# Experts of a two-block model on one core: where the row weights are copied, which buffers the block outputs use, and when the last norm's rows are loaded

## The chip, the cores and the metric

The kernel runs on one core of one Trainium2 chip, in one launch. The core has a matrix engine (TensorE; PE in the profile, PEld for its weight loads), VectorE (DVE), ScalarE (ACT), GpSimd (POOL), and SyncE (SP), which here only issues DMAs. Each engine takes its own instructions strictly in the order in which they stand in its queue; engines and DMAs wait for each other through semaphores. The metric is device time in microseconds, less is better. The kernel before took 4433.74 us (median of 3 runs, 4425.26 to 4436.02).

## The reference, cut to what matters

The model is an attention block of two layers, then a block with a token mixer, two layer norms and a mixture of experts over 1024 tokens of 1024 features. The change is in the experts and in the last norm:

```python
def _moe_ffn(h, router_w, router_b, w1, w3, w2, sw1, sw3, sw2):
    scores = jax.nn.sigmoid((h @ router_w).astype(f32))
    ...                                     # 64 experts, 8 chosen for each token
    wts = wts / jnp.sum(wts, -1, keepdims=True) * ROUTED_SCALE
    ...                                     # tokens sorted by expert, blocks of rows
    def body(acc, blk):
        tok, wt, e = blk
        xb = h[tok]                                            # gather rows
        hid = jax.nn.silu(xb @ w1[e]) * (xb @ w3[e])
        return acc.at[tok].add(wt[:, None] * (hid @ w2[e])), None   # scatter, weighted
    shared = (jax.nn.silu(h @ sw1) * (h @ sw3)) @ sw2
    return routed.astype(h.dtype) + shared

x = _layernorm(DN_ALPHA * x + g2 * f, ln2_w[l], ln2_b[l])      # the last norm
```

All tensors are float32. A product is done as three products of rounded parts (high times high, low times high, high times low), so each operand is first split in two on ACT and DVE.

## The kernel before, in words

The experts' part starts near 3176 us of the profiled span and ends it. Its work is a list of 105 blocks of up to 128 rows: 8 blocks of the shared expert, then 97 blocks of the 64 routed experts, whose capacities by falling count are fixed (`CAPS`); a loop at the end would do what exceeds them. For each routed block the kernel does these steps:

- `gather` (L2558 on): a one-hot comparison on DVE and eight small matmuls give the rows' token numbers `ix`; an indirect DMA, issued by POOL (L2575), brings the rows with their 64 weights by expert from `h_d` into `xg`.
- behind it, in `come` (L2697, L2698): POOL copies the weights' column out of `xg` into `wc`.
- `turn` (L2578): eight transposes on PE, and the split of the rows into `xh` and `xl`.
- `first` (L2595): the product with w1 and w3, silu, product `hid`. A block of at most 64 rows packs both parts of its rows into one product, and its two halves are added by way of a buffer `both` (L2605 to L2607) with the tag `ye`.
- `middle` (L2613): transposes `hid` and splits it.
- `second` (L2623): the product with w2; ACT writes it, times `wc`, into `y`, also of tag `ye` (L2631); POOL issues an indirect DMA that adds the rows to `acc_d` (L2635).

The tag `ye` has two buffers for both uses, `ix` has six, `xg` three. A tile that is allocated anew waits until everything that uses its buffer is done; for `ye` and `ix` that is the landing of the scatter that reads them. Two scatters in a row touch the same tensor `acc_d`, so each one also waits for the landing of the one before.

The steps of different blocks are interleaved by the loop at L2715: in turn i come the rows of block i + 3, `first` of block i, `turn` of block i + 1, seven splits of the next experts' weights, `second` of block i - 1 and `middle` of block i. This is the order of the program; the order in an engine's queue is set by a scheduler, which puts instructions where it reckons that they can run. Only SP keeps the program's order in this part (L2681). SP loads the experts' weights (three loads of 1 MB an expert) into four buffers `w_raw`.

The last norm needs the modulation's last part `g2` as a row on all partitions (eight transposes and two copies, `mod_row`), and the two vectors `ln2_w` and `ln2_b`. They are made in turn 3 of the loop, in buffers of the pool `rp`, which holds the first norm's rows till then. That pool stays open to the end.

Of the kernel before, what the change touches and what calls it, by code (L numbers as in the profile page):

```python
# [39 lines left out]
class K:  # L40
    """Engines, pools and constants that all phases share."""
# [23 lines left out]
    def psum(self, **bufs):  # L65
        """Banks by what they are for."""
        if self._ps:
            self._ps.close()
        self._ps = ExitStack()
        self.bufs = bufs or dict(mm=5, tr=2, po=1)  # L70
        self.ps = self._ps.enter_context(self.tc.tile_pool(name="ps", bufs=1, space=PSUM, reuse_waits="tile"))
# [7 lines left out]
    def rsqrt(self, out, in_, scale, eps):  # L79
        """out = (in_ * scale + eps) ** -0.5"""  # L80
# [8 lines left out]
    def split(self, hi, lo, src, scale=None, eng=None):  # L89
        """hi + lo = src (* scale, one number per partition), hi rounded as the tensor engine does."""  # L90
# [9 lines left out]
    def mm3(self, out, a, b, start, stop):  # L100
        """out += a^T b with both operands in two parts."""
# [6 lines left out]
    def mm_packed(self, both, top, a2, ah, bh, bl, start, stop):  # L108
        """both += a2^T bh and top += ah^T bl; a2 has the two parts of a side by side, top is both's first half,
        and the sum of both's halves is a^T b."""  # L110
# [8 lines left out]
    def vectors(self, pool, name, rows):  # L119
        """Vectors from DRAM (each a multiple of P long) as columns [P, n]: {key: column range}."""  # L120
# [16 lines left out]
    def bcast_row(self, out, col):  # L137
        """out[:, j] = col[j] for every partition: a column of P numbers as a row on all partitions."""
# [5 lines left out]
def vec(ap):  # L144
    """A DRAM vector (n * P,) as rows [n, P]."""
    return ap.rearrange("(n p) -> n p", p=P)


def gemv(k, pool, out, cs, w, b, ncols, chunk=128, group=4, tag="mm", ttag="tr", bufs=4):
    """out[:, j, :] = w[:, j * P:(j + 1) * P]^T cs + b[:, j], cs [P, KD, 2]; in steps."""  # L150
# [22 lines left out]
def run(gen, n=None):  # L173
    """The next n steps of a generator, or all that are left."""
    while n is None or n > 0:
        if next(gen, run) is run:
            return
        n = n and n - 1
# [42 lines left out]
def beside(main, side, n):  # L221
    """Steps of main, with n of side after every one."""
# [16 lines left out]
def put_h(k, wp, xn, tok, hh, hl, g, sh, onv=2):  # L239
    """(xn * g + sh) for a token tile, transposed and in two parts; onv of four features' tiles on the vector  # L240
    engine."""
# [20 lines left out]
def load_w(k, pool, w, c0, n, kt=KD, scale=None, tag="w", wmax=P, ktmax=KD, bufs=2, rbufs=2, rpool=None):  # L262
    """Columns c0..c0+n of w [kt * P, :] in two parts, [P, kt, n]."""
# [12 lines left out]
def head_weights(k, pool, I, l, pr, v, own=None):  # L276
    """Weights of a pair of heads' queries, and of its keys and values, in two parts, scaled by the norms'; in the
    places of the input product's weights, the parts in the pool own if there is one."""
# [15 lines left out]
class Columns:  # L294
    """Weights' tiles of P columns one after another, in turns in two pools; the first may be loaded ahead."""
# [12 lines left out]
def product(k, w, h, t0, n):  # L308
    """A bank with w^T h over n tokens from t0 on."""
# [7 lines left out]
def silu_out(k, sg, ps, dst):  # L317
    """silu(ps) into DRAM by way of sg."""
# [16 lines left out]
def block1(k, I, x_open, x_out, ahead, fill):  # L335
    """The first block: both layers; x_open(pool), then x_out(pool, t, tile) for the x token tiles, and
    what x_open returns, each of which returns what is to be done later; ahead: the next
    block's first weights, then a product with them; fill(pool): steps to be done beside the second layer's attention."""
    nc, tc = k.nc, k.tc
    A = nc.vector  # L340
    with ExitStack() as es:
# [16 lines left out]
        def early(pool=None):  # L358
            """The second layer's first weights, then a product with them."""
# [7 lines left out]
        def vectors(l):  # L367
            """The layer's vectors and tables."""
# [21 lines left out]
        def modulation(l, gp, **kw):  # L390
            """Shift and scale, then the gate."""
# [11 lines left out]
        def second(gp, **kw):  # L403
            """What the second layer needs."""
# [13 lines left out]
        def begin(wp):  # L418
            """The first layer's input."""
# [25 lines left out]
        for l in range(2):  # L445
# [26 lines left out]
            def weights():  # L472
                """In the place of what only the preparations need: the output's weights."""
# [15 lines left out]
def in_proj(k, I, l, last, h, vecs, keep, wp, ydram, sga_d, begin):  # L489
    """The layer's input product and its two convolution branches; begin(pool) makes the input."""  # L490
# [5 lines left out]
    with ExitStack() as es:  # L496
# [6 lines left out]
        def each(c0, n, cks, fn):  # L503
            """fn(feature tile, chunk of tokens, PSUM) over columns c0..c0+n of the input's product."""
# [6 lines left out]
        # queries' and keys' low-rank inputs in two parts, and the sums of their squares per token  # L511
# [16 lines left out]
        def to_tokens(sm, n):  # L528
            """Numbers per token in both rows of sm, on the tokens' partitions [P, n / P]; sm is used again."""
# [16 lines left out]
        # both segments with room for the taps that reach over their ends  # L546
# [9 lines left out]
        # conformer branch's input  # L556
# [12 lines left out]
        # the second layer's first ones have begun in the first layer  # L569
# [15 lines left out]
        def conformer():  # L585
            """Long convolution, layer norm over the features, pointwise product."""
# [23 lines left out]
        def pointwise(s):  # L610
            # mean and variance on all partitions
# [46 lines left out]
        # k_rope: both parts of the weights side by side, summed by tokens  # L658
# [28 lines left out]
        # gates of the attention's output  # L687
# [5 lines left out]
        # short convolution branch: gates, then the input  # L693
# [35 lines left out]
        def short():  # L729
            """The last product, and the convolution one chunk behind."""  # L730
# [11 lines left out]
def attention(k, I, l, last, v, hw, tabs, keep, fp, kp, ydram, sga_d, side, after):  # L742
    """All heads; side's steps beside the first one's preparation, after's beside the last two heads, when keep and
    the pools fp and kp aren't needed any more."""
    nc, tc = k.nc, k.tc
    lo_t = CT if last else 0
    with ExitStack() as es:
# [10 lines left out]
        # keys' shared part: norm weight, rotation, squares  # L758
# [7 lines left out]
        def rotate(eng, o, x, tb, tmp):  # L766
            """o = rotation of the pairs (x[j], x[16 + j]), o may be x; tb has the tables, tmp two buffers."""
# [2142 lines left out]
```

## Time and profile before

| what | value |
|---|---|
| median of 3 runs | 4433.74 us |
| span of the profiled execution | 4414.7 us |
| what lies around the span, against the median | 19.0 us |
| PE, DVE, ACT, POOL busy, of the span | 92%, 65%, 45%, 28% |
| stage of the routed blocks that is read below | 3300 to 4325 us |

The span runs from the first to the last instruction of the program; the page gives no other time for the profiled execution, so that the launch around it is taken as the difference to the median. A busy share says how long an engine had an instruction in work. POOL's 28% holds neither the time in which it waits for a DMA that it has issued nor the time for which those behind it in its queue are held up by that.

### The profile page before, as it was taken

What the parts mean: (1) busy time and instruction counts of PE and PEld (TensorE: products, weight loads), DVE (VectorE), ACT (ScalarE), POOL (GpSimd) and SP (SyncE); (2) the same over time, 40 slices, a digit from 0 to 9 for tenths busy, and PEclk for the clock granted to TensorE, in tenths of its full rate; (3) what the DMA queues carried; (4) which work ended last, traced back from release to release, by engine and by line L of the source; (5) the groups of instructions that cost most, each with busy time, mean ns of one, the idle gap of its engine ahead of it and who ended that gap; (6) DMA issues with size and microseconds to landing.
All of it is one profiled execution on the core that took longest, in us unless ns stands there. A gap on an engine that the chain in (4) does not pass through costs nothing. (4 is left out here: it accounts for less than half of the span.)

```text
span 4414.7 us, 61941 instructions
## 1 busy us (share of the span) xinstructions
PE 4045.3 (92%) x22375; PEld 3077.3 (70%) x22376; DVE 2878.1 (65%) x5659; ACT 1983.2 (45%) x4292; POOL 1231.9 (28%) x1211
## 2 busy tenths in 40 slices
PE   7999899999998999999997999999898898899993
PEld 5787666667776666788785788777776566666672
DVE  4684577764745778646764555667776676776775
ACT  4122366653112766423443133433256566666664
POOL 1201133332101333321334331122313333343233
PEclk9999999999999999999997999899999999999996
DMA  6121400123123001334434411215368888888885
GB/s 187 34 64 43 123 13 13 33 83 107 41 61 102 11 10 36 121 117 129 126 118 136 122 34 33 74 44 189 110 228 264 242 265 247 256 276 264 269 274 165
DMA packets 371316, 558.81 MB, mean 127 GB/s; under 512 B 52126, under 2 KB 285056, under 8 KB 346048
## 3 DMA queue, kind: packets, MB, share of 16 engines
q1 hardware_dynamic: 335728, 432.81, 30.5%
q0 software_dynamic: 35280, 122.02, 10.7%
q8 instruction: 177, 2.90, 0.3%
q14 instruction: 131, 1.07, 0.1%
HBM read 438.42 MB, written 116.33 MB: 126 GB/s over the span
## 5 line engine op out<-in xcount | busy, mean ns | idle before, releaser
L95 DVE TENSOR_TENSOR wa_lo<-w_raw,wa_hi 128x512 fp32r<-128x512 f32 x520 | 338.1, 685 | 18.6 <-ACT wa_hi L94 17.8
L94 ACT ACTIVATE wa_hi<-w_raw 128x512 fp32r<-128x512 f32 x520 | 299.7, 626 | 59.9 <-PE mm L106 24.9
L104 PE MATMUL mm<-hh,w_hi 128*128 128x512 f32 (+1 forms) x848 | 320.0, 377 | 4.7 <-ACT h L256 4.7
L105 PE MATMUL mm<-hl,w_hi 128*128 128x512 f32 (+1 forms) x848 | 318.7, 376 | 0.0
L106 PE MATMUL mm<-hh,w_lo 128*128 128x512 f32 (+1 forms) x848 | 317.1, 374 | 0.0
L104 PE MATMUL mm<-wa_hi,xh 128*128 128x512 f32 (+3 forms) x632 | 268.0, 424 | 2.8 <-ACT xh L94 2.7
L106 PE MATMUL mm<-wa_hi,xl 128*128 128x512 f32 (+3 forms) x632 | 259.4, 410 | 3.6 <-DVE xl L95 3.6
L105 PE MATMUL mm<-wa_lo,xh 128*128 128x512 f32 (+3 forms) x632 | 261.3, 414 | 1.2 <-DVE wa_lo L95 1.2
L892 DVE TENSOR_REDUCE mx<-mm 128x1 f32<-128x512 f32 (+1 forms) x400 | 225.1, 587 | 53.2 <-PE mm L891 50.7
L926 ACT ACTIVATE pe<-mm 128x512 f32<-128x512 f32 (+1 forms) x336 | 193.2, 588 | 144.3 <-PE mm L106 115.5
L931 POOL TENSOR_TENSOR pl<-pe,ph 128x512 fp32r<-128x512 f32 x96 | 142.0, 1482 | 335.4 <-ACT ph L930 326.5
L931 DVE TENSOR_TENSOR pl<-pe,ph 128x512 fp32r<-128x512 f32 (+1 forms) x240 | 204.6, 864 | 38.1 <-ACT ph L930 36.8
L2698 POOL COPY wc<-xg 128x1 f32<-128x1 f32 (+5 forms) x97 | 79.6, 820 | 508.4 <-DMA xg<-h_d,ix 502.3
L2635 POOL DMA_INDIRECT acc_d<-ye,ix x97 | 168.7, 1740 | 182.5 <-ACT hidh L94 73.4
L159 PE MATMUL mm<-gemv_w,b_c_cs 128*2 128x128 f32 x1536 | 199.0, 286 | 10.2 <-DMA gemv_w<-in_w_mod_dram 7.1
L2631 ACT ACTIVATE ye<-mm,wc 128x512 f32<-128x512 f32 (+5 forms) x194 | 127.6, 680 | 176.7 <-DMA acc_d<-ye,ix 125.1
L595 DVE SCALAR_TENSOR_TENSOR acc<-zc,b_v,acc 128x512 f32<-128x512 f32 (+1 forms) x300 | 199.3, 713 | 1.5
L104 PEld LDWEIGHTS mm<-hh,w_hi 128*128 128x128 f32 x848 | 161.3, 190 | 40.1 <-issue 7.6
L105 PEld LDWEIGHTS mm<-hl,w_hi 128*128 128x128 f32 x848 | 161.4, 190 | 33.8 <-issue 7.0
L94 ACT ACTIVATE w_hi<-w_raw 128x1024 fp32r<-128x1024 f32 x61 | 64.6, 1059 | 262.5 <-PE mm L105 227.2
L106 PEld LDWEIGHTS mm<-hh,w_lo 128*128 128x128 f32 x848 | 161.2, 190 | 28.1 <-issue 0.4
L930 ACT ACTIVATE ph<-pe 128x512 fp32r<-128x512 f32 (+1 forms) x296 | 178.0, 625 | 4.1
(779 smaller groups left out, 11572.8 us busy)
## 6 DMA issues: line engine op xcount, KB each, us to landing
w_raw<-in_exp_w_dram SPq DMA_DIRECT2D x192, 1024.0 KB
w_raw<-in_w_in_dram SPq DMA_DIRECT2D x69, 512.0 KB
gemv_w<-in_w_mod_dram SPq DMA_DIRECT2D x48, 512.0 KB
gemv_w<-in_ada_w_dram SPq DMA_DIRECT2D x48, 512.0 KB
rec<-rec SPq DMA_DIRECT2D x64, 256.0 KB
wo_raw<-in_w_out_dram SPq DMA_DIRECT2D x20, 512.0 KB
y<-ydram SPq DMA_DIRECT2D x36, 256.0 KB
xt<-in_x_dram SPq DMA_DIRECT2D x16, 512.0 KB
```

Of the source, the lines that this page charges most:

```text
L94: nc.scalar.activation(hi, src, AF.Copy)
L95: eng.tensor_tensor(lo, src, f32(hi), op=OP.subtract)
L104: mm(out, ah, bh, start=start, stop=False)
L105: mm(out, ah, bl, start=False, stop=False)
L106: mm(out, al, bh, start=False, stop=stop)
L159: nc.tensor.matmul(ps[:2, c0:c0 + chunk], cs[:, kk], wt[:, kk], start=kk == 0, stop=kk == KD - 1)
L595: nc.vector.scalar_tensor_tensor(o, zc[:, ft, p0 + j:p0 + j + c[1]], v["cfw"][:, 2 * j + ft:2 * j + ft + 1], o, op0=OP.mult, op1=OP.add)
L892: nc.vector.tensor_reduce(mx[:, t, c:c + 1], ps[:, :n], axis=AX.X, op=OP.max)
L926: nc.scalar.activation(pe, ps, AF.Exp)
L930: nc.scalar.activation(ph, pe, AF.Copy)
L931: (nc.gpsimd if j % PLP == PLP - 1 else nc.vector).tensor_tensor(pl, pe, f32(ph), op=OP.subtract)
L2635: nc.gpsimd.indirect_dma_start(out=self.acc_d, out_offset=bass.IndirectOffsetOnAxis(ap=st.ix[:n, 0:1], axis=0), in_=y[:n], in_offset=None, ...
```

## The change

The copy of the row weights `wc` moves in the program from `come`, behind the gather, to `turn`, two loop turns later. The block outputs `y` get a pool of their own with four buffers, at the place of the pool `rp`, which is closed as soon as the late steps of the output product are done; `ye` keeps its two buffers for `both` alone. `ix` gets eight buffers. `g2` and the last norm's two vectors are made behind the loop, in buffers of the second product's weights. The rest of the diff drops comments and docstrings.

```diff
     def experts(self, x1, out):
-            g2 = rp.tile([P, D], F32, name="g2", tag="sc2")
-            last = []
-            def beside_shared():
-                run(self.mod_row(g2, 5, "tr"))
-                last.extend((self.row(rp, "ln1w", I["ln2_w_2"][0]), self.row(rp, "ln1b", I["ln2_b_2"][0])))
...
-                st.ix = xp.tile([P, 1], I32, name="ix", bufs=6)
+                st.ix = xp.tile([P, 1], I32, name="ix", bufs=8)
...
             def turn(st):
                 n = st.n
+                if st.r is not None:
+                    st.wc = xp.tile([P, 1], F32, name="wc", bufs=6)
+                    nc.gpsimd.tensor_copy(st.wc[:n], st.x[:n, D + st.r:D + st.r + 1])
...
             def second(st):
-                y = xp.tile([P, D], F32, name="ye")
+                y = yp.tile([P, D], F32, name="y")
...
                     gather(b, self.routes[3][:, :, b.r:b.r + 1], b.base)
-                    b.wc = xp.tile([P, 1], F32, name="wc", bufs=6)
-                    nc.gpsimd.tensor_copy(b.wc[:b.n], b.x[:b.n, D + b.r:D + b.r + 1])
...
             next(late)
+            self.row_s.close()
+            yp = pool("y", 4, side="right")
             come(blocks[2])
...
                 run(route, 2)
-                if i == 3:
-                    beside_shared()
             ms.close()
             x = [wp.tile([P, D], F32, name="x", tag=("wa_hi", "wa_lo")[t % 2], bufs=8) for t in range(8)]
             for t in range(8):
                 k.load(x[t], self.x2_d[t * P:t * P + P])
+            g2, lw, lb = (wp.tile([P, D], F32, name=n, tag=g, bufs=4)
+                          for n, g in (("g2", "wb_hi"), ("lw", "wb_lo"), ("lb", "wb_lo")))
+            for a, n in ((lw, "ln2_w_2"), (lb, "ln2_b_2")):
+                k.load(a, I[n][0].unsqueeze(0).to_broadcast([P, D]))
+            run(self.mod_row(g2, 5, "tr"))
```

POOL's queue in the middle of the routed blocks, before (DMA xg is a gather, DMA acc_d a scatter, in brackets the semaphores that are waited for; DMASW ones are those of POOL's own DMAs):

```order
L2635 DMA acc_d<-ye,ix 1152x1024 [waits DMASW1_49,Activation_49]
L2575 DMA xg<-h_d,ix 32x1088 [waits DVE_49,PE_49,Pool_49]
L2635 DMA acc_d<-ye,ix 1152x1024 [waits DMASW3_49,Activation_49]
L2698 COPY wc<-xg 32x1 [waits DMASW4_49]
L2575 DMA xg<-h_d,ix 112x1088 [waits DVE_49,PE_49,Pool_49]
L2698 COPY wc<-xg 112x1 [waits DMASW6_49]
L2635 DMA acc_d<-ye,ix 1152x1024 [waits DMASW5_49,Activation_49]
L2575 DMA xg<-h_d,ix 128x1088 [waits DVE_49,PE_49,Pool_49]
L2698 COPY wc<-xg 128x1 [waits DMASW0_49]
```

And the same piece of POOL's queue now:

```order
L2629 DMA acc_d<-y,ix 1152x1024 [waits DMASW1_49,Activation_49]
L2566 DMA xg<-h_d,ix 32x1088 [waits DVE_49,PE_49,Pool_49]
L2629 DMA acc_d<-y,ix 1152x1024 [waits DMASW3_49,Activation_49]
L2574 COPY wc<-xg 32x1 [waits DMASW4_49]
L2566 DMA xg<-h_d,ix 112x1088 [waits DVE_49,PE_49,Pool_49]
L2574 COPY wc<-xg 112x1 [waits DMASW6_49]
L2629 DMA acc_d<-y,ix 1152x1024 [waits DMASW5_49,Activation_49]
L2566 DMA xg<-h_d,ix 128x1088 [waits DVE_49,PE_49,Pool_49]
L2574 COPY wc<-xg 128x1 [waits DMASW0_49]
```

Nothing has moved: the copy stands at the same place behind its own gather, and each scatter still waits for the landing of the one before. Over the whole part POOL's queue has the same order of gathers, copies and scatters as before.

ACT's queue at a packed block of 32 rows, before (ye<-mm at L2606 is `both`, ye<-mm,wc the block's output):

```order
L94 ACTIVATE wa_hi<-w_raw 128x512
L2606 ACTIVATE ye<-mm 32x512 [waits DMASW7_49,PE_49,Activation_49]
L94 ACTIVATE xh<-mm 128x4x112 [waits PE_49] x2
L94 ACTIVATE wa_hi<-w_raw 128x512 x2
L2610 ACTIVATE hid<-ye 32x256 [waits DVE_49]
L94 ACTIVATE wa_hi<-w_raw 128x512 x2
L2631 ACTIVATE ye<-mm,wc 128x512 [waits PE_49,DMASW1_49,Activation_49,Pool_49]
```

And the same now:

```order
L94 ACTIVATE wa_hi<-w_raw 128x512
L2600 ACTIVATE ye<-mm 32x512 [waits PE_49]
L94 ACTIVATE xh<-mm 128x4x112 [waits DVE_49,PE_49]
L94 ACTIVATE xh<-mm 128x4x112 [waits PE_49]
L94 ACTIVATE wa_hi<-w_raw 128x512 x2
L2604 ACTIVATE hid<-ye 32x256 [waits DVE_49]
L94 ACTIVATE wa_hi<-w_raw 128x512 x2
L2625 ACTIVATE y<-mm,wc 128x512 [waits DMASW3_49,PE_49,Pool_49]
```

The copy into `both` no longer waits for a scatter; the output waits for the scatter of four blocks before, where it was one or two blocks.

DVE's queue ahead of the first gather, before (posr are the positions from the router, g a row of the modulation, oh the one-hot rows of the first gathers):

```order
L2515 COPY posr<-mm 128x64 x8
L2389 COPY g_28053<-mm 128x512 x2
L2563 TENSOR_TENSOR oh<-c_iota,posr 128x1024 x2
L2809 TENSOR_TENSOR w_raw<-es,w_raw 128x64
L2812 SCALAR_TENSOR_TENSOR w_raw<-w_raw 128x64 x2
```

And now:

```order
L2506 COPY posr<-mm 128x64 x8
L2554 TENSOR_TENSOR oh<-c_iota,posr 128x1024 x2
L2806 TENSOR_TENSOR w_raw<-es,w_raw 128x64
L2809 SCALAR_TENSOR_TENSOR w_raw<-w_raw 128x64 x2
L2814 TENSOR_SCALAR w_raw<-w_raw 128x1
```

The two copies of `g2` are gone from there; they, the eight transposes, and on SP the two loads of the last norm's vectors stand at the end now, the loads behind those of `x`.

## Rows read from the trace of the kernel before

**Rows 1.** Stage 3300 to 4325: busy us of PE, PEld, DVE, ACT, POOL; clock, DMA share, GB/s.
```profile
3300.00:4325.00 1025.00, 914.46 (x4722) 681.99 (x4722) 717.88 (x1446) 641.92 (x1181) 362.30 (x274) 0.94 0.84 260
```

**Rows 2.** Waits of all engines, 3300 to 4325: us in total, times, longest.
```profile
POOL wc L2698 <- DMA xg<-h_d,ix: 455.3, 75, 10.5
ACT ye L2631 <- DMA acc_d<-ye,ix: 114.9, 31, 13.8
DVE ix L2573 <- DMA acc_d<-ye,ix: 97.8, 22, 8.2
...
PE mm L2620 <- DVE hid L2611: 56.2, 20, 7.5
...
ACT ye L2606 <- DMA acc_d<-ye,ix: 48.0, 13, 8.1
...
PE mm L2591 <- DVE hidl L95: 38.5, 5, 11.2
```

**Rows 3.** POOL by line, 3300 to 4325: busy us, mean ns, idle before.
```profile
L2635 POOL DMA_INDIRECT acc_d<-ye,ix x92 | 161.2, 1753 | 158.5 <-ACT hidh L94 63.9 <-ACT ye L2631 33.3 <-ACT ye L2606 27.0
L2575 POOL DMA_INDIRECT xg<-h_d,ix x91 | 132.2, 1453 | 42.4 <-issue 16.2 <-DVE xh L95 6.8 <-DVE ye L2607 5.5
L2698 POOL COPY wc<-xg 128x1 f32<-128x1 f32 (+5 forms) x91 | 78.3, 861 | 461.4 <-DMA xg<-h_d,ix 455.3 <-DVE wa_lo L95 6.1
```

**Rows 4.** Timeline of POOL, two stretches: start, length in us, idle before.
```profile
3878.06 1.49 POOL L2635 DMA_INDIRECT acc_d<-ye,ix  x1 [0.59 <-DVE ix L2573]
3879.86 3.25 POOL L2575 DMA_INDIRECT xg<-h_d,ix  x1 [0.30 <-issue]
3884.58 1.58 POOL L2635 DMA_INDIRECT acc_d<-ye,ix  x1 [1.48 <-ACT hidh L94]
3891.51 3.01 POOL L2698 COPY wc<-xg 96x1 f32<-96x1 f32 x1 [5.34 <-DMA xg<-h_d,ix]
...
4271.99 1.49 POOL L2635 DMA_INDIRECT acc_d<-ye,ix  x1 [0.62 <-ACT ye L2606]
4274.38 0.95 POOL L2575 DMA_INDIRECT xg<-h_d,ix  x1 [0.90 <-DVE hid L2611]
4279.67 1.97 POOL L2635 DMA_INDIRECT acc_d<-ye,ix  x1 [4.34 <-ACT wa_hi L94]
4281.11 2.67 POOL L2698 COPY wc<-xg 64x1 f32<-64x1 f32 x1
```

**Rows 5.** Tile xg, 3300 to 4325: landing of its gathers from their issue.
```profile
DMA to landing us min/median/max: 4.3/7.9/12.9
```

**Rows 6.** Tile wc, 3300 to 4325: the copy, ns min, median, max.
```profile
L2698 POOL COPY wc<-xg x91: 177/394/6247, 3308.0 to 4321.7; 128x1 f32<-128x1 f32 x40, 64x1 f32<-64x1 f32 x18, 96x1 f32<-96x1 f32 x11, 112x1 f32<-112x1 f32 x10
```

**Rows 7.** Timeline of DVE at the copy of 3891.51.
```profile
3890.32 1.88 DVE L95 TENSOR_TENSOR wa_lo<-w_raw,wa_hi 128x512 fp32r<-128x512 f32 x3
```

**Rows 8.** Timelines of DVE, SP and POOL about the first gather.
```profile
3223.08 1.29 DVE L2389 COPY g<-mm 128x512 f32<-128x512 f32 x2
...
3235.70 0.67 SPq L77 DMA_DIRECT2D ln1b<-in_ln_b_dram  x1
...
3246.86 0.18 POOL L2698 COPY wc<-xg 128x1 f32<-128x1 f32 x1 [9.49 <-DMA xg<-h_d,ix]
```

**Rows 9.** Line L2388 (transposes for g2) on PE, 3221 to 3234.
```profile
3221.00:3234.00 13.00, 1.36 (x8) 0.96 (x8) 1.00 0.12 25
```

**Rows 10.** DMA, 3232 to 3262.
```profile
DMA packets 2071, 10.50 MB, mean 350 GB/s; under 512 B 351, under 2 KB 351, under 8 KB 1247
```

**Rows 11.** Timelines of SP and POOL at the end.
```profile
4324.91 5.37 SPq L77 DMA_DIRECT2D x<-x_d  x8
...
4328.15 1.46 POOL L2635 DMA_INDIRECT acc_d<-ye,ix  x1 [4.19 <-DMA acc_d<-ye,ix]
4339.07 1.56 POOL L2635 DMA_INDIRECT acc_d<-ye,ix  x1 [9.46 <-ACT hidh L94]
...
4351.75 1.43 POOL L2635 DMA_INDIRECT acc_d<-ye,ix  x1 [4.35 <-DMA acc_d<-ye,ix]
```

More of the change, by code (lines that the diff above doesn't have):

```diff
@@ L2364, in experts @@
     def experts(self, x1, out):
-        I, rp = self.I, self.rp
         with self.tc.tile_pool(name="me_x", bufs=2, reuse_waits="tile") as xp, \
@@ L2371, in experts @@
             self.k.psum(**MPS)
-            g2 = rp.tile([P, D], F32, name="g2", tag="sc2")
-            last = []
-            def beside_shared():
-                run(self.mod_row(g2, 5, "tr"))
-                last.extend((self.row(rp, "ln1w", I["ln2_w_2"][0]), self.row(rp, "ln1b", I["ln2_b_2"][0])))
-            self.moe(xp, raw, late, beside_shared, lambda x, fp: self.last_norm(x, fp, raw, out, g2, *last))
-        self.row_s.close()
+            self.moe(xp, raw, late, lambda x, fp, *rows: self.last_norm(x, fp, raw, out, *rows))
     def mod_row(self, out, i, tag):
@@ L2518, in router, with moe @@
         self.routes = io, es, eid, posr
-    def moe(self, xp, raw, late, beside_shared, finish):
+    def moe(self, xp, raw, late, finish):
         k, nc, tc, I = self.k, self.nc, self.tc, self.I
@@ L2763, in moe @@
                 second(b)
-            finish(x, cp)
+            finish(x, cp, g2, lw, lb)
     def last_norm(self, xs, fp, raw, out, g2, lw, lb):
```

## Prediction

> **What bounds the kernel now.** I read the stages first. In the stage of the routed blocks PE is busy for 914.46 of 1025 us, at a granted clock of 0.94, so it does not run through [rows 1]. The waits say who stops it: PE waits 56.2 and 38.5 us for `hid` and `hidl` of DVE, DVE waits 97.8 us at `ix` for scatters, and ACT waits 114.9 and 48.0 us for scatters, at the block output and at the copy into `both` [rows 2]. So far it looks as if two buffers `ye` and six `ix` were too few.
>
> Then I asked why the scatters are late, and read POOL by line. Its copies `wc` stand idle for 461.4 us, its copies, gathers and scatters take 78.3, 132.2 and 161.2 us [rows 3]. Together that is 833 us of 1025 in which POOL works, or waits for a gather that it has itself just issued, with the next scatter locked in behind that wait. POOL's timeline shows the loop: scatter, 0.3 us later gather, wait for the landing (7.9 us from issue in the median [rows 5]), copy, about 0.6 us later the next scatter [rows 4]. The stage has 65 such turns and 26 pairs in which a second scatter stands between a gather and its copy; two pairs are in [rows 4]. The shortest gaps are 0.30 us ahead of a gather and 0.6 ahead of a scatter that follows a copy: 91 x 0.30 + 65 x 0.6 = 66 us. 833 + 66 = 899 us are thus fixed by POOL's queue alone.
>
> What remains is 15 us ahead of gathers (42.4 - 27.3) and 120 ahead of scatters (158.5 - 39) [rows 3]. The latter lie in the pairs. In the first pair shown the scatter waits 1.48 us and is issued by 3886.2, while the copy behind it waits for the gather till 3891.51: the scatter's wait costs nothing. In the second it waits 4.34 us, till 7.68 us after the scatter before it (4271.99), whose landing it needs anyway; its copy starts 6.7 us after the gather's issue, less than the median landing, so little is lost there too [rows 4]. My reading: POOL's queue sets the pace, and the waits of ACT, DVE and PE are its slack seen from the other side.
>
> **The change part by part.** *The copy.* The program moves it by two turns, but in the queue it stands where it stood, right behind its gather. It removes nothing: 0.
>
> *Four `y`, `both` for itself, eight `ix`.* The waits of ACT (114.9 + 48.0) and of DVE (97.8) for scatters should go [rows 2]. What is late next is the gather: blocks reach PE no faster than POOL brings them. On the path lies only what these waits did to POOL. Gathers that waited for `ix` and for DVE: at most the 15 us above, of which I take 7, since part of them wait for the transposes that free `xg`. Pairs in which the output came late: I take 2 of the 120 us, after the two pairs read. The bounds are far apart: if all of both went, 135 us; on the other side, were the copy's time doubled, a loss of 78.3 us [rows 3]. I stay near the pairs, since they show the wait itself. Stage: -9.
>
> The Trainium skill (Perfetto Trace Analysis, Optimization Strategy) says that the same gap again and again on the engine that should be saturated can mean too few buffers. By that rule PE's gaps would close; the trace agrees that buffers are what ACT waits for, and differs in that the buffers' release hangs on POOL's loop. It is the first rival below.
>
> *The last norm's rows.* Ahead of the first gather DVE loses two copies, 1.29 us [rows 8], and PE eight transposes, 1.36 us [rows 9]. The gather's index hangs on DVE and PE in turn, so I take 1 us. SP loses two loads of 0.5 MB each, the last issued at 3235.70, just ahead of that gather, whose copy then waited 9.49 us [rows 8]. At the 350 GB/s of that stretch [rows 10] 1.05 MB take 3.0 us; from 0 (the gather is hidden from them) to 3.0 I take 2. As POOL's loop starts with this gather, both count: -3, from 0 to -4.4.
>
> At the end the two loads follow the eight of `x` (5.37 us of SP for eight, so about 0.7 each), and nothing needs them before the sums behind the last scatter, issued at 4351.75 [rows 11]. The scatters 4328.15 to 4351.75, each waiting for the one before, hide them, the transposes and the copies; without that cover they would cost 3.0 + 1.3 + 1.4 = 5.7 us. One scatter there waited 9.46 us, for an output that itself waited for a scatter [rows 11]; with four buffers only the landing is left: -1, from 0 to -2.
>
> Sum: -9 - 3 - 1 = -13 us, 0.3%. The profiled execution spans 4414.7 us, 19.0 below the median of the runs; I put the same 19.0 around the new span of 4401.7, which gives **4421 us**.
>
> **The rivals.** *PE closes its gaps.* If POOL had room after all, because its waits come from blocks that are themselves held up, the gaps of PE for `hid` and `hidl`, 56.2 + 38.5 = 95 us [rows 2], would go: 4434 - 95 = 4339. For it: ACT's waits are plainly for buffers. Against it: the fixed 899 us and the unchanged queue. Chance 0.13.
>
> *It changes nothing.* What POOL gains here and there is given back by gathers that land later, since the DMA engines are busy for 0.84 of the stage [rows 1] and a landing varies from 4.3 to 12.9 us [rows 5]. 0.1 us on each of 91 gathers is 9 us. 4434, from 4425 to 4442. For it: 13 us is little against that spread. Against it: no reason why they should land later. Chance 0.25.
>
> *Slower, at the copies.* The copy has a median of 394 ns and a mean of 861, with a longest of 6247 [rows 3, 6]; one of 3.01 us begins in the middle of a run of DVE's `wa_lo` [rows 4, 7]. The long ones cost (861 - 394) x 91 = 42 us now. Without its 97.8 us of waits for scatters DVE may run longer in one piece just when a gather lands. With 143 ns more in the mean of a copy (13 us over 91) the gain is gone, and from twice that on it begins to be slower. With long copies that cost twice what they cost now it is 4421 + 42 = 4463, with half as much again 4421 + 21 = 4442. Against it: DVE does the same work in the same order. Chance 0.12.
>
> The Trainium skill (SBUF — State Buffer, Who interferes with whom) says that a DVE instruction with two inputs in SBUF and a GpSimd instruction that reads SBUF hold each other up for a whole instruction. `wa_lo` has two such inputs and the copy reads SBUF; the trace's long copies agree, and they are longer than one DVE instruction. By that rule alone the stage pays what it pays now, unless the runs meet the copies more often.
>
> **How the numbers follow.** My case, POOL's queue as the bound with a small gain, has 0.50, and its own range is 4405 to 4433 (the 15 us of gathers and 4.4 + 2 at the ends in full, some pairs besides, down to none). A measurement of this kernel can tell a change of about 0.3%, 13 us, from none, so faster means under 4420, slower over 4447. Half of my case is just below 4420, half above: faster 0.27 + 0.13 = 0.40; same 0.23 + 0.25 = 0.48; slower 0.12. The range for 8 in 10 goes to 4385, which leaves most of the first rival out (0.10), and to 4450, which leaves out the worse half of the third (0.06).
>
> **What would show it.** In the changed kernel's profile POOL's copy should still stand idle for some 450 us on the gather in the same stretch, the 65 turns and 26 pairs unchanged. ACT and DVE should show next to no wait for scatters, and PE, ACT or DVE longer ones for rows that a gather brings. The first gather should be issued 1 to 3 us earlier and land sooner. I am wrong if the copies' idle time shrinks to well under 400 us, if PE's busy share in the stage goes clearly above 0.92, or if the mean copy is over 1.0 us.

## The result: 4381 us, 1.0% less, and the profile after

The changed kernel took 4381.28 us (median of 4 runs, 4374.54 to 4396.88), the kernel before 4434.16 (4 runs, 4425.26 to 4436.02). The ratio is 0.9897, with a 95% interval of 0.9872 to 0.9923: faster by 1.0%, 34 to 57 us. Forecast were 4421, from 4385 to 4450, and 0.48 for no change that can be measured against 0.40 for faster. The ratio times 4434 gives 4388; the median itself lies 4 us under the range. The direction is the one that the sum had; the gain is three to four times its 13 us (42 us in the larger set of runs below, 53 between these medians).

The two profiled executions show only 20 us of it: spans of 4394.7 and 4414.7. Single executions differ by more than that. Beside the experiments below, 23 runs of the kernel before went from 4408.59 to 4441.19, and the changed kernel's from 4371.88 to 4399.49. So sizes are taken from medians, and the profiles say where.

The stage of the routed blocks after, in the columns of [rows 1]:

```profile
3300.00:4325.00 1025.00, 931.65 (x4815) 695.93 (x4813) 734.75 (x1456) 658.79 (x1195) 305.07 (x274) 0.95 0.86 266
```

PE works 17 us more of the same 1025, POOL 57 us less. The waits of that stage, in the columns of [rows 2]:

```profile
POOL wc L2574 <- DMA xg<-h_d,ix: 498.4, 77, 13.3
...
PE mm L2585 <- DMA xg<-h_d,ix: 85.0, 34, 6.4
...
POOL acc_d L2629 <- DMA acc_d<-y,ix: 75.7, 13, 8.2
```

All the waits of ACT and DVE for scatters in [rows 2] are gone, and so are PE's for `hid` and `hidl` (56.2 and 38.5 us). PE now waits 85.0 us for rows that a gather brings, and POOL 498.4 us for gathers (455.3 before). POOL by line, as in [rows 3]:

```profile
L2629 POOL DMA_INDIRECT acc_d<-y,ix x93 | 164.6, 1770 | 189.2 <-DMA acc_d<-y,ix 75.7 <-ACT wb_hi L94 29.7 <-ACT wa_hi L94 27.0
L2566 POOL DMA_INDIRECT xg<-h_d,ix x90 | 105.5, 1172 | 28.2 <-issue 20.3 <-POOL wc L2574 7.6 <-PE mm L2585 0.3
L2574 POOL COPY wc<-xg 128x1 f32<-128x1 f32 (+5 forms) x91 | 42.3, 465 | 498.4 <-DMA xg<-h_d,ix 498.4
```

The copy's mean fell from 861 to 465 ns, the gather's from 1453 to 1172; the idle time ahead of copies rose by 37 us and that ahead of scatters by 31. POOL's instructions got shorter, and POOL waits longer for DMAs of its own: 498.4 us for gathers, and 75.7 us ahead of a scatter for the one before it, a wait that the stage did not have before. The same from the copies themselves (ns min, median, max) and the gathers' landings, against [rows 6] and [rows 5]:

```profile
L2574 POOL COPY wc<-xg x91: 177/261/2992, 3304.3 to 4300.8; 128x1 f32<-128x1 f32 x40, 64x1 f32<-64x1 f32 x18, 96x1 f32<-96x1 f32 x11, 112x1 f32<-112x1 f32 x10
```

```profile
DMA to landing us min/median/max: 4.3/8.2/14.2
```

POOL's timeline of the first pair of [rows 4], the same block of 96 rows, with the scatter ahead of it; then the gather that ended that pair before, which [rows 4] do not show:

```profile
3853.20 1.93 POOL L2629 DMA_INDIRECT acc_d<-y,ix  x1 [0.63 <-ACT wa_hi L94]
3855.43 1.08 POOL L2566 DMA_INDIRECT xg<-h_d,ix  x1 [0.30 <-issue]
3861.57 1.97 POOL L2629 DMA_INDIRECT acc_d<-y,ix  x1 [5.06 <-DMA acc_d<-y,ix]
3864.60 0.18 POOL L2574 COPY wc<-xg 96x1 f32<-96x1 f32 x1 [1.06 <-DMA xg<-h_d,ix]
3865.34 0.96 POOL L2566 DMA_INDIRECT xg<-h_d,ix  x1 [0.56 <-POOL wc L2574]
```

```profile
3894.68 3.15 POOL L2575 DMA_INDIRECT xg<-h_d,ix  x1 [0.16 <-POOL wc L2698]
```

The second scatter of the pair (3861.57) now waits for the landing of the one before it, the copy takes 0.18 us instead of 3.01, and the next gather goes out 9.91 us after the pair's gather (3865.34 against 3855.43). Before, it went out 14.82 us after it (3894.68 against 3879.86).

The first two gathers before, and the first two with the copy between them now (against [rows 8]); then the end (against [rows 11]):

```profile
3236.30 1.07 POOL L2575 DMA_INDIRECT xg<-h_d,ix  x1 [2.07 <-DVE ix L2573]
...
3247.99 1.26 POOL L2575 DMA_INDIRECT xg<-h_d,ix  x1 [0.30 <-issue]
```

```profile
3237.02 1.07 POOL L2566 DMA_INDIRECT xg<-h_d,ix  x1 [2.29 <-DVE w_raw L2825]
3243.66 0.44 POOL L2574 COPY wc<-xg 128x1 f32<-128x1 f32 x1 [5.57 <-DMA xg<-h_d,ix]
3245.59 1.00 POOL L2566 DMA_INDIRECT xg<-h_d,ix  x1 [0.96 <-issue]
```

```profile
4311.30 1.46 POOL L2629 DMA_INDIRECT acc_d<-y,ix  x1 [8.24 <-DMA acc_d<-y,ix]
4317.69 1.56 POOL L2629 DMA_INDIRECT acc_d<-y,ix  x1 [4.94 <-DMA acc_d<-y,ix]
4326.44 1.42 POOL L2629 DMA_INDIRECT acc_d<-y,ix  x1 [7.19 <-DMA acc_d<-y,ix]
4331.79 1.43 POOL L2629 DMA_INDIRECT acc_d<-y,ix  x1 [3.93 <-DMA acc_d<-y,ix]
```

From the first gather to the second it is 8.57 us now and was 11.68. The points in time themselves can't be compared: in three executions with this order (this one, and two of the experiments below, the change again and the buffers of before) the first gather starts at 3237.0, 3233.8 and 3231.1, while the distance to the second is 8.57, 8.56 and 8.56. The last scatters follow each other's landings, none waits for an output.

### The profile page after: what moved, and what is told of

Its sections match the earlier page's. It is cut to its first block, busy times and chain, and to the rows that moved or that the text cites. A ratio compares the mean times of both kernels' runs of the same rounds, so it can differ in the third digit from the quotient of the medians.

```text
span 4394.7 us, 61923 instructions
## 1 busy us (share of the span) xinstructions
PE 4042.7 (92%) x22376; PEld 3080.2 (70%) x22376; DVE 2889.0 (66%) x5659; ACT 1992.9 (45%) x4292; POOL 1172.9 (27%) x1211
## 5 line engine op out<-in xcount | busy, mean ns | idle before, releaser
L104 PE MATMUL mm<-wa_hi,xh 128*128 128x512 f32 (+3 forms) x632 | 257.6, 408 | 0.0
L105 PE MATMUL mm<-wa_lo,xh 128*128 128x512 f32 (+3 forms) x632 | 251.7, 398 | 1.2 <-DVE wa_lo L95 1.2
L2629 POOL DMA_INDIRECT acc_d<-y,ix x97 | 171.3, 1766 | 201.7 <-DMA acc_d<-y,ix 86.9
L2585 PE MATMUL mm<-ident,xg 128*128 128x128 f32 (+5 forms) x840 | 119.4, 288 | 85.0 <-DMA xg<-h_d,ix 85.0
L104 PE MATMUL mm<-wb_hi,hidh 128*128 128x512 f32 (+5 forms) x420 | 188.8, 450 | 0.0
L2585 PEld LDWEIGHTS mm<-ident,xg 128*128 128x128 f32 (+5 forms) x840 | 109.1, 198 | 111.2 <-issue 99.1
L2574 POOL COPY wc<-xg 128x1 f32<-128x1 f32 (+5 forms) x97 | 44.0, 454 | 534.6 <-DMA xg<-h_d,ix 534.6
```

The lines of the kernel that those rows point to most:

```text
L104: mm(out, ah, bh, start=start, stop=False)
L105: mm(out, ah, bl, start=False, stop=False)
L2585: nc.tensor.transpose(ps[:, j * n:(j + 1) * n], xk[:, 4 * q + j], k.ident[:n, :n])
L2629: nc.gpsimd.indirect_dma_start(out=self.acc_d, out_offset=bass.IndirectOffsetOnAxis(ap=st.ix[:n, 0:1], axis=0), in_=y[:n], in_offset=None, ...
```

## The experiments

In all of them the ratio is to runs of the kernel before on the same chip (median 4422 to 4428); the changed kernel's time to compare with is that of the next run, 4380. Theory A is the prediction's: POOL's queue, with its wait behind each gather, sets the pace, and the buffers matter only by what they do to that queue. Theory B: the buffers gain by themselves, because outputs and `ix` no longer wait for scatters. A variant of A, that the buffers only shorten POOL's copies, came up on the way.

**The change again.**

> The changed kernel once more, beside the others on the same chip and with more runs. The two profiled executions differ by 20 us (4414.7 and 4394.7), the medians of the runs by 53. If the runs tell the change's size, this comes out 40 to 55 us faster than before, and its profile shows a loop part (from the fifth scatter to the last gather) some 40 us shorter than 990. If the profiles tell it, it comes out 15 to 25 faster and the loop part is 970 to 975.

Median 4379.85, ratio 0.9905 (0.9881 to 0.9928); its profiled span is 4369.7 and the loop part (from the gather ahead of the fifth scatter to the last gather) 951 us, against 992 before and 973 in the first profile of the changed kernel. The runs are right: the change is worth 42 us.

**The buffers of before, the rest of the change kept.**

```diff
-                y = yp.tile([P, D], F32, name="y")
+                y = xp.tile([P, D], F32, name="ye")
-                st.ix = xp.tile([P, 1], I32, name="ix", bufs=8)
+                st.ix = xp.tile([P, 1], I32, name="ix", bufs=6)
```

> The changed kernel with the buffers of before: outputs and halves in two shared buffers ye, six ix. Every engine has the changed kernel's order; what is left of the change is the copy's place in the program and the last norm's rows at the end. If the buffers make the gain, it is within 5 us of before (4425 to 4435). If moving the last norm's rows away from the first gather makes it, as much as 20 to 50 us of the gain stays. My prediction gave the rows 4 us in all.

Median 4423.96, ratio 1.0001 (0.9988 to 1.0013). The last norm's rows and the copy's place in the program are worth nothing that can be measured; the buffers make all of the gain. The old waits are back (this and the lines of the next experiments are from 3300 to 4250 where nothing else is said), and so are the long copies and the idle time ahead of gathers:

```profile
ACT ye L2625 <- DMA acc_d<-ye,ix: 111.6, 25, 13.5
DVE ix L2564 <- DMA acc_d<-ye,ix: 76.3, 16, 7.6
```

```profile
L2566 POOL DMA_INDIRECT xg<-h_d,ix x84 | 116.3, 1384 | 46.8 <-issue 12.2 <-DVE wa_lo L95 7.9 <-DVE xh L95 7.8
L2574 POOL COPY wc<-xg 128x1 f32<-128x1 f32 (+5 forms) x84 | 67.9, 809 | 433.5 <-DMA xg<-h_d,ix 433.5
```

**Each kind of buffer by itself.**

```diff
-            yp = pool("y", 4, side="right")
+            yp = pool("y", 2, side="right")
```

> The changed kernel with two buffers for the outputs instead of four; the halves keep buffers of their own, ix eight. Order of every engine unchanged. If the pairs of scatters make the gain because an output waits for the landing of a scatter one or two blocks before, an output with two buffers still waits for the scatter of two blocks before, and at least half of the gain is lost (time within 20 us of before). If it is DVE's wait at ix that costs, or the halves, the gain stays whole (within 8 us of the changed kernel).

Median 4412.22, ratio 0.9972 (0.9958 to 0.9987): 12 of 42 us left.

```diff
-                st.ix = xp.tile([P, 1], I32, name="ix", bufs=8)
+                st.ix = xp.tile([P, 1], I32, name="ix", bufs=6)
```

> The changed kernel with six ix buffers instead of eight; four outputs as changed, order of every engine unchanged. If the outputs' buffers make the gain, it keeps all but 10 us of it (4375 to 4392). If DVE's wait at ix for a scatter's landing (97.8 us before) is what costs, because it then runs its backlog of wa_lo beside POOL's copies and gathers, DVE waits some 100 us there again, the mean copy is near 0.8 us again, and at least half of the 42 us goes (4400 or more).

Median 4408.75, ratio 0.9974 (0.9960 to 0.9988): 11 us left. So neither alone will do: with two outputs ACT waits for scatters, with six `ix` DVE does, and either waits longer than it did before. The waits, of the kernel with two outputs, with its POOL copies by line:

```profile
ACT y L2625 <- DMA acc_d<-y,ix: 201.0, 57, 9.7
```

```profile
L2574 POOL COPY wc<-xg 128x1 f32<-128x1 f32 (+5 forms) x85 | 50.3, 592 | 457.0 <-DMA xg<-h_d,ix 454.2 <-DVE oh L2554 1.6 <-DVE ic L2562 1.3
```

and of the one with six `ix`, likewise:

```profile
DVE ix L2564 <- DMA acc_d<-y,ix: 166.4, 40, 10.5
```

```profile
L2574 POOL COPY wc<-xg 128x1 f32<-128x1 f32 (+5 forms) x84 | 77.9, 927 | 440.8 <-DMA xg<-h_d,ix 435.1 <-PE mm L2614 5.7
```

**Is POOL's queue the bound? The copy twice.**

```diff
                     nc.gpsimd.tensor_copy(st.wc[:n], st.x[:n, D + st.r:D + st.r + 1])
+                    nc.gpsimd.tensor_copy(st.wc[:n], st.x[:n, D + st.r:D + st.r + 1])
```

> The changed kernel with the copy of the row weights done twice in a row on POOL. The second copy takes 0.2 to 0.5 us each with its start, 97 times. If POOL's queue (gather, wait, copy, scatter) sets the pace of the changed kernel, 20 to 45 us are added (4400 to 4425). If PE, the DMA engines or the serial scatters set it, nothing measurable is added (within 8 us of the changed kernel).

Median 4413.01, 33 us above the changed kernel (ratio to before 0.9982, 0.9965 to 0.9999). The second copies took 392 ns each:

```profile
L2575 POOL COPY wc<-xg 128x1 f32<-128x1 f32 (+5 forms) x82 | 32.1, 392 | 5.1
```

97 x 0.392 = 38 us on POOL make 33 us of time. POOL's queue sets the pace of the changed kernel.

**The copy on ACT, behind the transposes in the program.**

```diff
-                    nc.gpsimd.tensor_copy(st.wc[:n], st.x[:n, D + st.r:D + st.r + 1])
...
+                    nc.scalar.activation(st.wc[:n], st.x[:n, D + st.r:D + st.r + 1], AF.Copy)
```

> The changed kernel with the copy of the row weights on ACT, behind the block's transposes in the program, so that nothing on POOL waits for a gather's landing and POOL's queue alternates scatter and gather. If POOL's queue is the bound (498 us of the stage it waits for a gather), the stage falls until scatters in series (landing 7.5 us, issue 1.6, 0.8 between: about 10 us a block against 10.9 now) or PE bind: 40 to 90 us faster than the changed kernel, 4290 to 4340. If PE with its clock, or the DMA engines at 0.86, bind already, it stays within 10 us of the changed kernel. If ACT then waits for gathers in POOL's place and holds up PE, it is slower than the changed kernel.

Median 4355.70, ratio 0.9837 (0.9817 to 0.9858): 24 us below the changed kernel, less than A asked for. The scheduler put these copies ahead of others of ACT's work, and ACT took over a part of the wait:

```profile
ACT wc L2587 <- DMA xg<-h_d,ix: 170.7, 47, 9.1
```

The same with the buffers of before:

> The buffers of before (outputs and halves in two ye, six ix) with the copy of the row weights on ACT, so that POOL never waits for a gather. If POOL's wait for gathers is the root and the two buffers only its slack, as my prediction had it, this is as fast as the same with four buffers: 4350 to 4375. If the lock of an output on the landing of a scatter one or two blocks before binds by itself, it stays near before: 4400 to 4430. In between, each is worth its share.

Median 4343.60, ratio 0.9824 (0.9806 to 0.9842): with POOL free of the wait, the old buffers are no slower than the new ones. That goes against B. Another bound that hides what the buffers are worth isn't seen in these two, first the one with the new buffers, then the one with the old, in the columns of [rows 1]:

```profile
3300.00:4250.00 950.00, 883.03 (x4597) 662.05 (x4596) 706.66 (x1413) 629.02 (x1237) 277.46 (x178) 0.96 0.88 276
```

```profile
3300.00:4250.00 950.00, 900.92 (x4734) 674.54 (x4733) 725.21 (x1454) 645.11 (x1279) 281.86 (x183) 0.97 0.90 283
```

PE still stands idle for 67 and 49 of the 950 us, and the DMA engines are busy for 0.88 and 0.90 of them.

**The copy on DVE, tied to the transposes** (`A` is VectorE).

```diff
-                    nc.gpsimd.tensor_copy(st.wc[:n], st.x[:n, D + st.r:D + st.r + 1])
...
+                    A.scalar_tensor_tensor(st.wc[:n], ps[:n, 0:1], 0.0, st.x[:n, D + st.r:D + st.r + 1],
+                                           op0=OP.mult, op1=OP.add)
```

> The changed kernel with the row weights taken by one DVE instruction that also reads the block's last transposes in PSUM (times zero), so that no engine waits for a gather but PE, which needs its rows. The kernel with the copy on ACT was 24 us faster than the changed one, and ACT waited 170 us at the copy for gathers. If that wait held up ACT's splits and through them PE, this is another 10 to 40 us faster: 4315 to 4345. If the DMA engines (0.88 of the stage) or the scatters in series bind by now, it is the same as with ACT: 4348 to 4362. If 97 small instructions more on DVE cost more than the wait did, it is slower than that.

Median 4292.53, ratio 0.9704 (0.9681 to 0.9727), 87 us below the changed kernel and better than expected. What this edit adds is 97 instructions of 142 ns; what it takes away is every wait for a gather but PE's own. A stretch of 900 us within the stage, of the kernel before and of this one, in the columns of [rows 1]:

```profile
3300.00:4200.00 900.00, 795.00 (x4113) 593.95 (x4113) 626.94 (x1263) 558.93 (x1026) 316.24 (x239) 0.94 0.84 261
```

```profile
3300.00:4200.00 900.00, 875.78 (x4716) 661.86 (x4715) 730.74 (x1536) 645.58 (x1177) 280.60 (x181) 0.99 0.94 296
```

PE is busy 876 of 900 us, at a granted clock of 0.99 instead of 0.94, and the DMA engines 0.94 of the time. A PE instruction's busy time fell from 193 ns in the mean (795.00 us by 4113) to 186 (875.78 by 4716). Which of PE and the DMA engines bounds this kernel was not tried.

**The move that the change's words describe.** The copy stays on POOL but also reads a number of the block's split rows, so that it can't run before these are there.

```diff
-                    nc.gpsimd.tensor_copy(st.wc[:n], st.x[:n, D + st.r:D + st.r + 1])
...
+                    nc.gpsimd.tensor_scalar(st.wc[:n], f32(st.xl[:n, 7, 0:1]), 0.0,
+                                            st.x[:n, D + st.r:D + st.r + 1], op0=OP.mult, op1=OP.add)
```

> The changed kernel with the copy still on POOL, but made to read a number of the block's split rows (times zero) as well, so that it can't run before the rows are turned. In POOL's queue it now stands two gathers behind its own: the move that the change's text describes and that the order did not show. If POOL's wait for the landing right behind its own gather was the bound, most of the gain of the copy on DVE (4293) is had here too: 4290 to 4330, the upper end if the copies' own 40 us on POOL still count. If POOL now waits as long for the splits of DVE as it did for the gather, it stays within 15 us of the changed kernel (4365 to 4395).

Median 4285.95, ratio 0.9685 (0.9667 to 0.9703). That is 4 us under the lower end of what was expected. In the queue 95 of the 97 copies now stand two gathers behind their own. POOL waits 43 us for splits where the changed kernel's waited 454 in the same 900 us for gathers (waits of the changed kernel, then of this one, then by line, all 3300 to 4200):

```profile
POOL wc L2574 <- DMA xg<-h_d,ix: 454.0, 70, 13.3
```

```profile
POOL wc L2587 <- DVE xl L95: 40.9, 21, 5.6
POOL wc L2587 <- DVE xh L95: 2.4, 4, 1.6
```

```profile
L2587 POOL TENSOR_SCALAR wc<-xl,xg 128x1 f32<-128x1 f32 (+3 forms) x67 | 91.9, 1372 | 42.7 <-DVE xl L95 40.9
```

The copies are three times as long as in the changed kernel (1372 ns for those of `xl`), and the kernel is no slower than the one with the copy on DVE: POOL has time again.

**The copy on DVE with the buffers of before.**

> The copy on DVE as in the fastest kernel so far, with the buffers of before (outputs and halves in two ye, six ix). If the four buffers are worth something only because of what their waits do to POOL's queue, they are worth nothing here: 4283 to 4302, as with four. If an output that waits for the landing of a scatter one or two blocks before binds by itself now that a block takes about 10 us, 20 to 60 us are lost: 4313 to 4353.

Median 4286.63, ratio 0.9684 (0.9670 to 0.9698): four outputs and eight `ix` are worth nothing here. The waits of ACT and DVE for scatters fell with the old buffers too, from 238 us of these 900 to 60, once POOL was free. The largest that is left costs nothing that can be measured:

```profile
ACT ye L2625 <- DMA acc_d<-ye,ix: 42.1, 19, 10.3
```

**Do the buffers only shorten POOL's copies?** A memset in the copy's place on POOL, the weights taken on DVE; with the buffers of before and with the new ones. The column that the memset writes is read by nobody.

```diff
-                    nc.gpsimd.tensor_copy(st.wc[:n], st.x[:n, D + st.r:D + st.r + 1])
...
+                    c = D + (st.r + 1) % 64
+                    nc.gpsimd.memset(st.x[:n, c:c + 1], 0.0)
```

> The buffers of before, the row weights taken on DVE behind the transposes, and on POOL, in the copy's place behind each gather, a memset of one column of the gathered rows that nobody reads. POOL thus still waits for each gather, but reads nothing in SBUF there. The POOL copies of before have a mean of 0.81 to 0.88 us and a shortest of 0.18. If it is the copies' length (held up beside runs of wa_lo) that the buffers of before cost, and the memset is not held up (mean near 0.2), 97 x 0.6 = 58 us go: 4355 to 4385. If the memset is held up as the copy was (mean 0.8), or if the locks of outputs and ix on scatters cost by themselves, it stays near before: 4410 to 4430.

> The same memset in the copy's place with the changed kernel's buffers. The copies there have a mean of 0.47 us, so that a memset of 0.2 gives 97 x 0.27 = 26 us: 4345 to 4365. If the buffers gain through the copies alone, this and the one with the buffers of before are within 12 us of each other; if through the outputs and ix by themselves, this one is 30 us or more faster than that one.

With the buffers of before: median 4411.75, ratio 0.9974 (0.9958 to 0.9991). With the new ones: 4377.36, 0.9895 (0.9869 to 0.9922), 12 us above the expected range. The memsets are short in both, so the copies' length is worth 12 us with the old buffers and nothing with the new; the buffers still gain 34 us beside it. The variant falls: while POOL waits behind each gather, the outputs and `ix` gain by themselves, as B has it; once that wait is gone they gain nothing, as A has it. Gathers and memsets of the first and then of the second, by line:

```profile
L2566 POOL DMA_INDIRECT xg<-h_d,ix x83 | 110.4, 1330 | 70.4 <-DVE wa_lo L95 16.8 <-issue 10.2 <-DVE ye L2604 8.8
L2574 POOL MEMSET xg<- 128x1 f32 (+5 forms) x83 | 16.6, 200 | 424.4 <-DMA xg<-h_d,ix 415.9 <-DVE wc L2590 4.4 <-DVE wa_lo L95 4.2
```

```profile
L2566 POOL DMA_INDIRECT xg<-h_d,ix x87 | 98.3, 1130 | 29.5 <-issue 20.0 <-POOL xg L2574 9.5
L2574 POOL MEMSET xg<- 128x1 f32 (+5 forms) x87 | 17.5, 202 | 467.1 <-DMA xg<-h_d,ix 464.0 <-DVE oh L2554 2.2 <-PE mm L106 0.8
```

The idle time ahead of the gathers shows where: 70.4 us with the old buffers, 29.5 with the new. Where the copy is short, the gather behind it waits for the other engines instead.

**Where in POOL's loop the buffers gain.** From POOL's timelines I took, for each pair in the loop part (fifth scatter to last gather), the time from the start of the copy behind the second scatter to the end of the next gather, and the landing of that gather and of the gathers in the plain turns, all from issue. The last column is the median of the runs. With six `ix` the trace lacks many of the landings. The two kernels with the memset have 28 pairs, the others 26.

| kernel | copy and next gather | pair's gather lands | turns' gathers land | time |
|---|---|---|---|---|
| before | 3.79 us | 7.52 | 8.20 | 4422 to 4434 |
| buffers of before | 3.58 | 7.40 | 8.15 | 4424 |
| memset, buffers of before | 3.30 | 7.64 | 8.24 | 4412 |
| six `ix` | 3.60 | | | 4409 |
| two outputs | 2.36 | 9.47 | 7.76 | 4412 |
| the change | 1.99 | 10.00 | 7.75 | 4381 |
| the change again | 1.98 | 9.75 | 7.46 | 4380 |
| memset, new buffers | 1.91 | 10.30 | 7.39 | 4377 |

In 26 pairs the change saves 26 x 1.80 = 47 us behind the second scatter. The gather that goes out there lands 2.2 to 2.5 us later, which costs 58 to 64 us. In both kernels it goes out while the second scatter is under way (24 of 26 times before, always now), but that scatter's landing is then 3.4 us away in the mean before, and 7.7 and 7.5 in the two executions now; that this is why the gather is late is argued, not tried. The 62 turns get their gathers 0.45 to 0.74 us sooner, 28 to 46 us. The sum is -11 for the one execution and -35 for the other; their loop parts are 18 and 41 us shorter than that of before.

The same without a choice of terms, from the issue of a gather to the issue of the next: with a second scatter between them 11.74 us before, 10.42 and 10.20 now (26 times); the others 11.08 before, 11.33 and 11.06 now (62 times). So the place is the pairs: they give 34 and 40 us, and the other turns take 16 or give 1. Which of the locked engines delays the next gather there, ACT by the output or DVE by `ix`, I can't separate: either lock alone costs 29 to 32 of the 42 us. For the kernel with two outputs the table explains only a part of its loss.

## Why the prediction was right in the bound and wrong in the size

**The bound: right.** That POOL's queue sets the pace, and that the waits of ACT, DVE and PE are its slack, was read from the order of POOL's instructions and the 461.4 us ahead of the copies. The doubled copy (+33 us), the copy moved off its gather (94 us less than the changed kernel, with the data dependence on POOL) and the old buffers beside a free POOL (no loss) show it.

**The copy: right.** It stood where it stood, and gave nothing. The prediction stopped there. Had it asked what a real move would give, the 461.4 us were the answer's upper end.

**The buffers: the failed step.** "I take 2 of the 120 us, after the two pairs read", and "at most the 15 us above" for the gathers. The term of 9 us measured 42. Both bounds were idle times of POOL, and I priced a pair by the wait ahead of its second scatter alone. What follows in the same rows is a copy of 3.01 us, and a gather of 3.25 stands ahead [rows 4]; these count as busy, and I took them as given. After the change they took 0.18 and 1.08 us in the same pair, and the whole pair 9.91 us instead of 14.82. With the old buffers a long copy hides that the next gather would have to wait: make it short and 70 us of idle time stand ahead of the gathers instead of 47. Busy time of an engine can cover a wait as well as idle time can show one. The outer bound of 135 us that I named had room for it; I went to the wrong end.

**Slower, at the copies: the wrong sign.** The mean copy should have risen if DVE ran longer in one piece. It fell to 465 ns. The two kernels with one kind of buffer agree with that: 592 ns where DVE has no waits for scatters, 927 ns where it waits 166.4 us. That DVE then runs off a backlog in one piece is the likely link, not shown. This term was there, 42 us for the long copies, but only as a danger; the memsets show that it is worth 12 us at most.

**PE closes its gaps: the waits moved, as argued.** The 95 us for `hid` and `hidl` went, 85.0 us for gathers came. The Trainium skill (Perfetto Trace Analysis, Optimization Strategy) says that the same gap again and again on the engine that should be saturated can mean too few buffers. The runs agree in part: more buffers gave 42 us. One instruction moved off POOL's wait gave about 140 us with the old buffers (4428 to 4287), and made more of them needless.

**Nothing changes: half true.** Gathers of the pairs do land later, by 2.2 to 2.5 us. I had seen no reason; the likely one, not tried, is that more of the second scatter is still to come when they go out (7.7 us to its landing instead of 3.4).

**The last norm's rows: -4 predicted, not measurable.** The ratio of the kernel with the old buffers, 1.0001, leaves 5 us either way, so 4 us can't be told from none. The term for the loads was right in kind: the second gather follows the first after 8.57 us instead of 11.68, 3.1 us less where I took 2 of at most 3.0. That the first gather is issued earlier can't be read, since executions differ there by 6 us. At the end, 99.5 us lay from the last gather to the end of the span before, and 99.7 after.

**The signs named beforehand** came as the prediction's bound would have them: 498.4 us of idle time ahead of the copies (some 450 said), PE busy for 0.91 of the stage (not above 0.92), a mean copy of 465 ns (not above 1.0 us), PE waiting for gathered rows, the order of POOL's queue unchanged. They speak for the bound, and couldn't tell a gain of 13 us from one of 42.

**The 19.0 us around the span were none.** Each run's record has its span and its time, and they differ by 1.8 to 2.2 us. What I took for a launch was the spread between executions. It stood on both sides of the sum, and so did no harm to the difference.

## What to carry to other kernels

An instruction that waits for a DMA, in the queue of the engine that issues the DMAs, holds up every later issue until the landing: here 455 of 1025 us, for a copy whose median is 0.4 us. Look for it in the engine's order, not in its busy share, and tie the instruction to work that comes after the landing, or give it to an engine that waits there anyway. Moving a line in the program doesn't move it where a scheduler can pull it forward again; a data dependence does. Buffers that wait for such a queue look like the bound, and are worth what they give back to the queue: try the queue first.

## What the runs showed of the hardware

A POOL copy that reads SBUF is held up for long beside DVE, a memset at the same place hardly: 809 ns in the mean for the copy with the buffers of before, 200 for the memset, with these extremes (ns min, median, max):

```profile
L2574 POOL COPY wc<-xg x84: 177/530/5267, 3300.3 to 4244.8; 128x1 f32<-128x1 f32 x38, 64x1 f32<-64x1 f32 x16, 112x1 f32<-112x1 f32 x10, 96x1 f32<-96x1 f32 x8
```

```profile
L2574 POOL MEMSET xg<- x83: 88/99/696, 3306.9 to 4242.1; 128x1 f32 x38, 64x1 f32 x15, 112x1 f32 x10, 96x1 f32 x8
```

The Trainium skill (SBUF — State Buffer, Who interferes with whom) says that a DVE instruction with two SBUF inputs contends with a GpSimd instruction that reads SBUF, and not with one that only writes it. These rows agree. From 3300 us on, 54 of the 91 copies begin while DVE runs a split `wa_lo` or `wb_lo` and take 1.12 us in the mean, the other 37 take 0.43; of the memsets 52 begin so and take 0.27 us, the other 39 take 0.14.

The hold can outlast one DVE instruction, and so be longer than the prediction's "a whole instruction". The copy of 3.01 us in [rows 4] begins at 3891.51, when the third of the `wa_lo` of [rows 7] starts, and ends at 3894.52, 0.04 us after the second of the two `wb_lo` that follow:

```profile
3892.13 2.35 DVE L95 TENSOR_TENSOR wb_lo<-w_raw,wb_hi 128x1024 fp32r<-128x1024 f32 x2
```
